# Three gated tiles with fewer convolution steps between them, the rest of the steps and the second output weight's split behind the last

## The chip, the cores and the metric

The kernel runs on one core of a Trainium2 chip. The metric is the device time of one execution in microseconds (us). The kernel before takes 1291.76 us, the median of three runs (1290.92 to 1293.04).

In this document PE is TensorE (the matrix engine), DVE is VectorE, ACT is ScalarE, POOL is GpSimd, and SP is the engine whose queue issues the loads and stores. "L553" is line 553 of the kernel.

## What is computed

A backbone of two layers works on 1024 tokens of width 1024. The change lies in the first layer, which has two branches behind one input projection, and one output projection behind both:

```python
z = h @ p["w_in"]
va, vg, ga, xb, gb = jnp.split(z, [W_CONV, 2 * W_CONV, 3 * W_CONV, 3 * W_CONV + W_LRU], axis=-1)
y_a = conformer_conv(va, vg, p) * jax.nn.silu(ga)      # 31 taps along the tokens, then a layernorm
y_b, hT = rglru_branch(xb, p, h0, True)                # two linear recurrences along the tokens
y_b = y_b * jax.nn.silu(gb)
return jnp.concatenate([y_a, y_b], axis=-1) @ p["w_out"], hT
```

The second layer (a pooling mixer) and the final norm follow. All of it is in 32-bit floating point, with each matrix product done as three products of a high and a low part (high by high, high by low, low by high).

## The kernel before, in words

**Tiles.** Channels lie on the 128 partitions, tokens along the free axis, so an activation of 1024 channels is 8 tiles (KT = 8) of 128 x 1024, and work goes by halves of 512 tokens. A weight tile is 128 x 1024: loaded raw from memory (`raw_load`, L579, by SP), rounded to its high part `wh` on ACT (`cast`), and subtracted to its low part `wl` on POOL (`gp`); both are in `raw_split` (L584). There are two buffers each for raw, high and low weights. A raw buffer comes free when POOL has made the low part from it.

**The stage of the change.** When the last recurrence has been scanned, its result for each tile n lies in memory (`yb_raw`). PE computes the gate products gb (weights gb4 to gb7 in this stage), 48 matmuls each (`gb_product`). ACT applies SiLU to each half (`gb_silu`, tiles `sb`). Then `gated(n, between)` (L1071) does, for each of the two halves of tile n: SP loads the half of the recurrence's result (`yr`, two buffers, so the load of a half waits until the multiplication two halves earlier is done); DVE multiplies it into the SiLU'd gate (`sb<-yr,sb`); ACT rounds the product to its high part (`ybh`); POOL subtracts to the low part (`ybl`); and DVE does `between` steps of the convolution (`fill(between)`). In this text half (n,h) is half h of tile n.

**The convolution's steps.** The convolution branch's 31 taps are DVE instructions, most of them `conv<-u,sm,conv`, cut into steps by a generator (`conv`, L617). Nothing but DVE is needed for them until the layernorm, so the code strews them between other work by `fill(n)`, n steps at a time. Seven steps follow each half of each output product (L1191), and before the last but one product is left, all steps still open are done (L1172), since the layernorm's mean needs all eight tiles.

**The output product.** From L1161 PE multiplies the gated tiles by the output weights wob0 to wob7, in order. Each is 24 matmuls per half: for each k of the 8 gated tiles, high weight by `ybh`, high weight by `ybl`, low weight by `ybh`. For wob0 the order is: k = 0 to 6 of half 0 (21 matmuls), k = 0 to 6 of half 1 (21), then k = 7 of half 0 and of half 1 (3 each). Its results leave by ACT (`wo`), are added on POOL to x (`xp`), and stored (`x_part`). After that come the layernorm, the products `ga` (gates of the convolution branch), and the second half of the output projection.

**What sets the order.** In this stage the order on PE, DVE, ACT and POOL is that of the program: each instruction is told to be issued behind the one before it on its engine (`on`, L549). The loads and stores on SP have no such order; a planner places them when it builds the program, by its own simulated time. From L1223 (`fixed[0] = False`) on, the order on all engines is the planner's.

The weights are split ahead of their use: in the loop at L1090, `gb_weights(j + 2)` splits gb6 and gb7 at j = 4 and 5, wob0 at j = 6 and wob1 at j = 7. The call stands ahead of `gated(j - 1)`, so the split of wob1 lies on ACT and POOL between the halves of tile 5 and those of tile 6.

Of the kernel before, what the change touches and what calls it, by code (L numbers as in the profile page):

```python
# [20 lines left out]
KT = D // P  # L21
# [35 lines left out]
def body(ctx, tc, xT, ctxT, cc, ccol, modT, modW, win, gw, wout, wu, grp, wg, wo1, small, edge, ident, outT):  # L57
# [501 lines left out]
    def cast(dst, src):  # L559
        return on("act", nc.scalar.copy, dst, src)  # L560

    def gp(*args, **kw):
        return on("pool", nc.gpsimd.tensor_tensor, *args, **kw)
# [15 lines left out]
    def raw_load(src, name):  # L579
        raw = wpool.tile([P, D], F32, tag="wr", name=f"wr_{name}")  # L580
        nc.sync.dma_start(raw, src)
        return raw

    def raw_split(raw, name):  # L584
        hi = wpool.tile([P, D], F32R, tag="wh", name=f"wh_{name}")
        lo = wpool.tile([P, D], F32R, tag="wl", name=f"wl_{name}")
        cast(hi, raw)
        gp(out=lo, in0=raw, in1=hi.bitcast(F32), op=sub)
        return hi, lo
# [14 lines left out]
    def vec(f, **kw):  # L604
        return on("vec", f, **kw) if fixed[0] else f(**kw)
# [56 lines left out]
    def ln_sums():  # L662
        for j in range(summed[0], ended[0]):
            for h in range(2):
                first = us[0][:, HALF[h]] if j == 1 else lnacc[h][:, :H]
                vec(nc.vector.tensor_tensor, out=lnacc[h][:, :H], in0=first, in1=us[j][:, HALF[h]], op=add)
        summed[0] = max(summed[0], ended[0])
# [24 lines left out]
    def fill(n):  # L692
        while n > 0:
            try:
                next(going[0])
                n -= 1
            except StopIteration:
                if begun[0] >= whole_[0]:
                    return
                going[0] = conv(begun[0])  # L700
                begun[0] += 1

    with ExitStack() as actx:
# [181 lines left out]
        def gb_weights(j):  # L885
            src, name = ((win[4 * KT + j], f"gb{j}") if j < KT else
                         (wout[j - KT, 1], f"wob{j - KT}") if j < 2 * KT else
                         (win[2 * KT + (0, KT // 2)[j - 2 * KT]], f"ga{(0, KT // 2)[j - 2 * KT]}"))
            gws[j] = raw_split(raw_load(src, name), name)

        def gb_product(j, w):
            if j == 4:
                gps[j] = (lambda t: [t[:, h] for h in HALF])(wide(f"gb{j}"))
            else:
                gps[j] = [psum(f"gb{j}_{h}") for h in range(2)]
            for h in range(2):
                all_of(mm3_fixed(gps[j][h], w, (hh, hl), HALF[h]))
# [3 lines left out]
        def gb_silu(j):  # L901
            sbs[j] = [ttile(f"sb{j}_{h}") for h in range(2)]
            for h in range(2):
                act(sbs[j][h], gps[j][h], AF.Silu)
# [32 lines left out]
    def d2tile(name, dt=F32):  # L937
        return d2pool.tile([P, S], dt, tag="d2", name=name)
# [5 lines left out]
    def vtile(name):  # L944
        return vpool.tile([P, H], F32, tag="v", name=name)
# [125 lines left out]
    def gated(n, between):  # L1071
        th, tl = d2tile(f"ybh{n}", F32R), d2tile(f"ybl{n}", F32R)
        for h in range(2):
            y = vtile(f"yr{n}_{h}")
            nc.sync.dma_start(y, yb_raw[n][:, HALF[h]])
            v = sbs[n][h]
            vec(nc.vector.tensor_tensor, out=v, in0=y, in1=v, op=mult)
            cast(th[:, HALF[h]], v)
            gp(out=tl[:, HALF[h]], in0=v, in1=th[:, HALF[h]].bitcast(F32), op=sub)
            fill(between)  # L1080
        bh.append(th)
        bl.append(tl)
# [7 lines left out]
    for j in range(3, KT + 1):  # L1090
        if j < KT:
            gb_silu(j)
        if 3 < j < KT:
            gb_weights(j + 2)
        if 3 < j < KT - 2:
            gb_product(j + 2, gws[j + 2])
        gated(j - 1, (0, 0, 4, 5, 5, 5, 3, 0)[j - 1])
        ln_sums()


# [809 lines left out]
```

## Time and profile before

| | |
|---|---|
| time, median of three runs | 1291.76 us |
| the profiled execution's own time | 1292.27 us |
| its span in the profile | 1290.5 us (1.77 us lie around it) |
| PE busy | 1264.4 us, 98% of the span |
| DVE busy | 1133.6 us, 88% |
| ACT, POOL busy | 648.8 us, 290.7 us |

A profile's page gives busy times of the engines. Further views of the trace are: the timeline, one row for each run of like instructions (start, duration, engine, line, what is written from what, count, and in brackets how long the engine had been idle and what released it); the table by stretches (busy time of each engine in a stretch of the span, with counts); the waits (who waited for whom, in all, how often, the longest); and the chain of waits that ended last, followed back from the last instruction. Helper functions record nearly all instructions of this stage under L553, so rows are told apart by the names of their tiles.

PE's matmuls are pipelined: where nothing holds them, their starts in this stage are 0.227 us apart, though each row shows a duration of 0.39 us.

### The profile page before, as it was taken

Reading aid. Unit: us, or ns where it says so; the run is one execution under the profiler, and the core shown is the slowest. Engines: PE = TensorE matmul, PEld = TensorE weight load, DVE = VectorE, ACT = ScalarE, POOL = GpSimd, SP = SyncE. Lnnn points to the kernel's source line nnn. Section 1 sums busy time; section 2 is a strip of 40 time slices with the busy share of each in tenths; the row PEclk is TensorE's granted clock in tenths of the full one; section 3 lists DMA queues with packets and bytes.
Section 4 is the critical chain, followed back from the end, with each engine's and each line's share of the span. In section 5 each row is a group of like instructions: output and inputs, shape, how many; then the busy total and the mean of one; then the engine's idle time right before and its main releaser. Section 6 shows DMA issues by size and latency. Waiting matters only on the chain.

```text
span 1290.5 us, 16117 instructions
## 1 busy us (share of the span) xinstructions
PE 1264.4 (98%) x5824; PEld 1040.4 (81%) x5824; DVE 1133.6 (88%) x1760; ACT 648.8 (50%) x939; POOL 290.7 (23%) x147
## 2 busy tenths in 40 slices
PE   9999999999999999999999999999999999999996
PEld 7788888888888887888887788787878888788785
DVE  6899999999999999969868959998999987887776
ACT  8555566656656533237434346644333444644542
POOL 0003464436443566434200032000000000000003
PEclk9999999999999999999999999999999999999998
DMA  9961121112111234442418566234333334868633
GB/s 374 396 211 49 42 74 43 64 41 74 57 66 57 82 115 137 143 137 82 163 50 285 173 212 177 92 123 155 117 115 120 115 122 131 298 225 281 212 110 130
DMA packets 78783, 182.33 MB, mean 141 GB/s; under 512 B 7664, under 2 KB 23408, under 8 KB 78704
## 3 DMA queue, kind: packets, MB, share of 16 engines
q1 hardware_dynamic: 70256, 177.12, 40.1%
q10 hardware_dynamic: 8448, 4.20, 1.1%
q8 instruction: 45, 0.74, 0.2%
q14 instruction: 34, 0.28, 0.1%
HBM read 137.24 MB, written 44.04 MB: 140 GB/s over the span
## 4 chain that ended last, share of the span: by engine, by line
PE 49%; DVE 31%; DMA 12%; issue 4%; ACT 3%; POOL 1%; SPq 0%; POOLq 0%; DVEq 0%; ACTq 0%
DVE conv L553 7%; PE wob L553 6%; PE vg L553 5%; PE va L553 5%; PE xb L553 4%; PE fold L123 3%; DVE l L553 3%; PE g L553 3%; DMA yr_t<-y_t 2%; DVE ws L1420 2%; DMA wr_v<-wfold 2%; PE ga L145 2%; PE ga L553 2%; PE ga L144 2%; PE ga L146 2%
## 5 line engine op out<-in xcount | busy, mean ns | idle before, releaser
L553 DVE SCALAR_TENSOR_TENSOR conv<-u,sm,conv 128x505 f32<-128x505 f32 (+6 forms) x224 | 153.5, 744 | 1.0
L1652 POOL TENSOR_TENSOR o<-x,rr 128x256 f32<-128x256 f32 (+1 forms) x10 | 9.9, 1022 | 448.7 <-ACT rr L1652 446.8
L553 ACT ACTIVATE l<-g,sm 128x512 f32<-128x512 f32 (+1 forms) x96 | 58.7, 619 | 57.8 <-PE g L553 57.0
L553 POOL TENSOR_TENSOR l<-l,l 128x1280 f32<-128x1280 f32 x16 | 47.1, 2966 | 25.6 <-DVE conv L553 14.1
L553 PE MATMUL wob<-ybl,wh_wob 128*128 128x512 f32 x128 | 50.2, 392 | 2.3 <-POOL ybl L553 2.3
L123 PE MATMUL fold<-gh,wh_wu 128*128 128x512 f32 x128 | 51.1, 399 | 1.2 <-ACT wh_wu L103 1.2
L103 ACT CAST wq_g<-wr_g 128x512 fp32r<-128x512 f32 x48 | 28.2, 620 | 46.6 <-DMA wr_g<-wg 15.0
L123 PE MATMUL fold<-gh,wl_wu 128*128 128x512 f32 x128 | 50.2, 395 | 0.5 <-DVE wl_wu L104 0.5
L553 PE MATMUL gb<-h0h,wl_gb 128*128 128x512 f32 x128 | 49.9, 390 | 0.3 <-POOL wl_gb L553 0.3
L123 PE MATMUL fold<-gl,wh_wu 128*128 128x512 f32 x128 | 50.1, 391 | 0.0
L553 PE MATMUL va<-h0h,wl_va 128*128 128x512 f32 x128 | 49.9, 390 | 0.1
L553 PE MATMUL vg<-h0h,wl_vg 128*128 128x512 f32 x128 | 49.9, 390 | 0.0
L553 PE MATMUL wob<-ybh,wl_wob 128*128 128x512 f32 x128 | 49.8, 389 | 0.0
L553 PE MATMUL gb<-h0l,wh_gb 128*128 128x512 f32 x128 | 49.8, 389 | 0.0
L553 PE MATMUL gb<-h0h,wh_gb 128*128 128x512 f32 x128 | 49.8, 389 | 0.0
L553 PE MATMUL va<-h0l,wh_va 128*128 128x512 f32 x128 | 49.8, 389 | 0.0
L553 PE MATMUL va<-h0h,wh_va 128*128 128x512 f32 x128 | 49.8, 389 | 0.0
L553 PE MATMUL wob<-ybh,wh_wob 128*128 128x512 f32 x128 | 49.8, 389 | 0.0
L553 PE MATMUL vg<-h0h,wh_vg 128*128 128x512 f32 x128 | 49.8, 389 | 0.0
L553 PE MATMUL vg<-h0l,wh_vg 128*128 128x512 f32 x128 | 49.8, 389 | 0.0
L553 DVE TENSOR_TENSOR_SCAN l<-l,l 128x256 f32<-128x256 f32 (+1 forms) x32 | 48.7, 1522 | 1.1
L553 DVE SCALAR_TENSOR_TENSOR conv<-cL,wsum,conv 128x506 f32<-128x506 f32 (+3 forms) x70 | 48.1, 744 | 0.2
(596 smaller groups left out, 4272.5 us busy)
## 6 DMA issues: line engine op xcount, KB each, us to landing
wr_wu<-wu SPq DMA_DIRECT2D x16, 512.0 KB, 4.2
modw<-modW SPq DMA_DIRECT2D x16, 512.0 KB, 10.2
x_part<-xp SPq DMA_DIRECT2D x32, 256.0 KB, 2.3
mod<-modT SPq DMA_DIRECT2D x32, 256.0 KB, 3.7
wr_v<-wfold SPq DMA_DIRECT2D x16, 512.0 KB, 4.1
wr_g<-wg SPq DMA_DIRECT2D x16, 512.0 KB, 4.8
wr_wo<-wo SPq DMA_DIRECT2D x16, 512.0 KB, 4.5
yr_t<-y_t SPq DMA_DIRECT2D x16, 512.0 KB, 5.8
```

The source lines that it names most:

```text
L103: return (nc.scalar.copy(hi, src), eng.tensor_tensor(out=lo, in0=src, in1=hi.bitcast(F32), op=sub))
L123: m = nc.tensor.matmul(*args, **kw)
L144: mm(ps, hi[:, kc], xh[k][:, cols], start=(k == 0), stop=False)
L145: mm(ps, hi[:, kc], xl[k][:, cols], start=False, stop=False)
L146: mm(ps, lo[:, kc], xh[k][:, cols], start=False, stop=(k == ks - 1))
L553: last[eng] = f(*args, **kw)
L1420: nc.vector.tensor_tensor(out=nxt[:, :, a_:b_], in0=cur[:, :, a_ + o0 : b_ + o0], in1=cur[:, :, a_ + o1 : b_ + o1], op=add)
L1652: tail[eng] = f(*args, **kw)
```

## The change

```diff
     for j in range(3, KT + 1):
         if j < KT:
             gb_silu(j)
-        if 3 < j < KT:
+        if 3 < j < KT - 1:
             gb_weights(j + 2)
         if 3 < j < KT - 2:
             gb_product(j + 2, gws[j + 2])
-        gated(j - 1, (0, 0, 4, 5, 5, 5, 3, 0)[j - 1])
+        gated(j - 1, (0, 0, 4, 5, 5, 3, 1, 0)[j - 1])
+        if j == KT:
+            gb_weights(KT + 1)
+            fill(8)
         ln_sums()
```

Three steps instead of five follow each half of tile 5, one instead of three each half of tile 6: eight steps fewer. Behind the last half of tile 7 stand the load and split of wob1 (which were ahead of tile 6) and the eight steps. Nothing is computed that was not computed before, and nothing is left out; the instructions' number on each engine stays the same.

## The prediction

> **What bounds the kernel now.** I read the page first, then the table by stretches around the stage of the change, then the waits, then the timelines of PE, DVE, ACT, POOL and SP from 485 to 512 us, and last the chain behind it. The page and the table:
>
> ```profile
> span 1290.5 us, 16117 instructions
> PE 1264.4 (98%) x5824; PEld 1040.4 (81%) x5824; DVE 1133.6 (88%) x1760; ACT 648.8 (50%) x939; POOL 290.7 (23%) x147
> ...
> 440.00:499.70 59.70, 59.43 (x262) 48.89 (x262) 57.60 (x82) 20.49 (x32) 29.21 (x17) 1.00 0.36 115
> 499.70:512.00 12.30, 10.01 (x42) 7.30 (x41) 12.09 (x19) 4.16 (x6) 8.24 (x7) 1.00 0.36 116
> 512.00:675.00 163.00, 163.00 (x720) 134.91 (x720) 132.76 (x202) 69.89 (x105) 52.99 (x29) 1.00 0.35 117
> ```
>
> The columns of the table are the stretch, its length, then busy time of PE, weight loads, DVE, ACT, POOL, and the granted clock. PE is the bound: 59.43 of 59.7 us before the start of the output product's trouble, and 163.00 of 163.00 behind it. Between the two lie 12.3 us in which it is busy for 10.01. The waits of 440 to 540 us name what it waits for, and PE's timeline shows where:
>
> ```profile
> PE wob L553 <- POOL ybl L553: 2.3, 3, 1.6
> ```
>
> ```profile
> 495.69 0.39 PE L553 MATMUL wob<-ybh,wh_wob 128*128 128x512 f32 x1
> 499.77 0.39 PE L553 MATMUL wob<-ybh,wh_wob 128*128 128x512 f32 x1
> 501.75 0.50 PE L553 MATMUL wob<-ybl,wh_wob 128*128 128x512 f32 x1 [1.59 <-POOL ybl L553]
> 507.14 0.39 PE L553 MATMUL wob<-ybh,wh_wob 128*128 128x512 f32 x1
> 507.94 0.50 PE L553 MATMUL wob<-ybl,wh_wob 128*128 128x512 f32 x1 [0.42 <-POOL ybl L553]
> 509.19 0.51 PE L553 MATMUL wob<-ybl,wh_wob 128*128 128x512 f32 x1 [0.28 <-POOL ybl L553]
> 511.82 0.39 PE L553 MATMUL wob<-ybh,wh_wob 128*128 128x512 f32 x1
> ```
>
> Number the matmuls of the output product. The one at 495.69 is the 1st; the one at 499.77 is the 19th (k = 6 of half 0, high by high). Eighteen pitches in 4.08 us are 0.2267 us each. The 20th needs the low part of half (6,0) and starts at 501.75 instead of 500.00. The 43rd (k = 7) starts at 507.14; by the pitch it would have been 495.69 + 42 x 0.2267 = 505.21, so the first wait has cost **1.93**. The 44th and 47th wait for the low parts of (7,0) and (7,1). The 58th, at 511.82, would have been at 508.61: **3.21 us** are lost in all, 1.28 of them by the last two waits. This is more than the 2.3 us of idle, because the matmuls behind each wait also start at a wider spacing for a while. 3.21 us is all that the stage has to give.
>
> **Why the low parts are late.** The rows of DVE (the `sb` rows are the multiplications of halves (5,1), (6,0), (6,1) and, two in one row, (7,0) and (7,1)), then ACT, then POOL:
>
> ```profile
> 489.07 3.51 DVE L553 SCALAR_TENSOR_TENSOR conv<-u,sm,conv 128x511 f32<-128x511 f32 x5
> 492.49 0.74 DVE L553 TENSOR_TENSOR sb<-yr,sb 128x512 f32<-128x512 f32 x1
> 493.15 3.35 DVE L553 SCALAR_TENSOR_TENSOR conv<-u,sm,conv 128x508 f32<-128x508 f32 x5
> 496.42 0.68 DVE L553 TENSOR_TENSOR sb<-yr,sb 128x512 f32<-128x512 f32 x1
> 497.02 2.30 DVE L553 SCALAR_TENSOR_TENSOR conv<-u,sm,conv 128x507 f32<-128x507 f32 x3
> 499.24 1.34 DVE L553 TENSOR_TENSOR sb<-yr,sb 128x512 f32<-128x512 f32 x1
> 500.50 1.23 DVE L553 SCALAR_TENSOR_TENSOR edge_junk<-u,sm 128x8 f32<-128x8 f32 x1
> 501.76 1.73 DVE L553 TENSOR_TENSOR u<-u 128x512 f32<-128x512 f32 x1
> ...
> 505.18 1.29 DVE L553 TENSOR_TENSOR sb<-yr,sb 128x512 f32<-128x512 f32 x2
> ```
>
> ```profile
> 495.95 0.60 ACT L553 ACTIVATE sb<-gb 128x512 f32<-128x512 f32 x1 [1.57 <-PE gb L553]
> 496.44 1.04 ACT L553 CAST wh_wob<-wr_wob 128x1024 fp32r<-128x1024 f32 x1
> 497.39 0.62 ACT L553 CAST ybh<-sb 128x512 fp32r<-128x512 f32 x1
> ```
>
> ```profile
> 497.62 2.40 POOL L553 TENSOR_TENSOR wl_wob<-wr_wob,wh_wob 128x1024 fp32r<-128x1024 f32 x1 [2.36 <-ACT wh_wob L553]
> 499.97 2.98 POOL L553 TENSOR_TENSOR ybl<-sb,ybh 128x512 fp32r<-128x512 f32 x2
> 506.60 2.53 POOL L553 TENSOR_TENSOR ybl<-sb,ybh 128x512 fp32r<-128x512 f32 x2 [3.65 <-ACT ybh L553]
> ```
>
> The first wait is the second weight's: its cast (1.04) stands on ACT ahead of `ybh` of (6,0), and its subtraction (2.40) on POOL ahead of `ybl` of (6,0), which so starts at 499.97 and not near 497.1. The other two are the convolution's: three steps, the last of them spread over 500.50 to 505.18, hold the multiplication of (7,0) until 505.18, so its low part starts at 506.60.
>
> **The change, walked through.** Up to 489.07 nothing moves. A step is 3.51 / 5 = 0.70 us, a multiplication takes about 0.65 of DVE's time. All times below are estimates from the rows above.
>
> DVE: three steps to 491.2, multiplication of (5,1) to 491.8, three steps to 493.9, (6,0) to 494.5, a step to 495.2, (6,1) to 495.9, a step to 496.6. Then a wait that was not there before: `yr` of (7,0) can be loaded only when (6,0) has freed its buffer.
>
> ```profile
> DMA to landing us min/median/max: 2.5/2.8/4.3
> ```
>
> ```profile
> 483.37 0.33 SPq L581 DMA_DIRECT2D wr_wob<-wout  x1
> 491.45 0.33 SPq L581 DMA_DIRECT2D wr_wob<-wout  x1
> ...
> 510.86 0.33 SPq L1107 DMA_DIRECT2D x_part<-xp  x1
> ```
>
> The first row is that of the `yr` tile: 2.8 us from issue to landing, 4.3 at most. So (7,0) starts at 494.5 + 2.8 = 497.3 and ends at 498.0; (7,1), whose load is issued at 495.9, starts at 498.7 and ends at 499.4 (with two slow loads, 500.9). DVE stands idle for 0.7 + 0.7 us (2.9 with slow loads). Behind the waiting multiplications stand only convolution steps, for which nobody waits before 560 us. On SP the load at 491.45 (the third weight, held there for its buffer) is ahead of 491.8, so it does not hold the `yr` loads up.
>
> ACT: the SiLU at 495.95 waits for PE's last gate product, as now; the next instruction starts at 496.45, and this is now `ybh` of (6,0), done at 497.05; (6,1) at 497.6, (7,0) at 498.65, (7,1) at 500.05, then the second weight's cast, to 501.1.
>
> POOL, at 1.30 us a half (2.53 / 2 rounded up): (6,0) from 497.1 to 498.4, (6,1) to 499.7, (7,0) to 501.0, (7,1) to 502.3, then the second weight's low part, 2.40, to 504.7.
>
> PE, without a wait: low of (6,0) asked for at 500.00 (1.6 us spare), (7,0) at 505.4 (4.4 spare), (7,1) at 506.1 (3.8 spare), the second weight's high part at 506.6 (5.5 spare), its low part at 507.0 (2.3 spare). With the slow `yr` loads (7,1)'s low part ends near 502.9 and the weight's at 505.3, still 1.7 early. **So all three waits go: -3.21.**
>
> The second weight's raw load is issued at 483.37 now, when its buffer comes free. The change leaves the buffer's time as it is, but the planner may put the load later on SP. Behind the last `yr` load it would be issued near 496.3, land 3.9 us later by this tile's median (row below), and be cast by 501.3: POOL comes free for it only at 502.3. From nothing to nothing, then; I take zero.
>
> ```profile
> DMA to landing us min/median/max: 3.4/3.9/4.8
> ```
>
> **The moved steps.** Eight steps of 0.70 are 5.6 us of DVE work, done 5 to 15 us later, plus 1.4 to 2.9 us of new idle. DVE works without a gap until the convolution ends, and then:
>
> ```profile
> 566.69 3.37 DVE L553 TENSOR_TENSOR ml_mu<-lnsum,mh_mu 128x512 fp32r<-128x512 f32 x2 [9.92 <-ACT mh_mu L553]
> ...
> 654.68 0.69 DVE L1277 TENSOR_TENSOR u<-u,ga 128x512 f32<-128x512 f32 x1 [4.14 <-ACT ga L1275]
> ```
>
> The steps cost nothing, because this idle of 9.92 us stands at their end. PE asks 3.2 us sooner and DVE arrives up to 2.9 later, so 3.8 or more remain. If that cover were gone, each microsecond beyond it would be a microsecond of PE. Behind that point DVE follows PE again (the 4.14 at 654.68 waits on a SiLU of a product of PE), and the chain of waits runs over PE alone from 509 to here, and then through ACT and DVE instructions that this matmul releases:
>
> ```profile
> 674.57 0.24 PE ga L145
> ```
>
> So what PE gains at 509 us is still there at 675, and the work behind starts as much earlier.
>
> **A rule weighed against the rows.** The multiplication of (6,1) takes 1.34 us beside a POOL subtraction, where that of (6,0) takes 0.68; `u<-u`, which reads two tiles, takes 1.73. The change packs four subtractions, two multiplications and a weight's subtraction together. If each waits for the other's end here, as those rows suggest, the order is: (6,0) low to 498.4, multiplication (7,0) to 499.1, (6,1) low to 500.4, multiplication (7,1) to 501.1, (7,0) low to 502.4, (7,1) low to 503.7, the weight to 506.1, or 506.8 with `u<-u` between. PE asks at 507.0. The sum stays 3.2, but with 0.2 us to spare instead of 2.3; it is the ground of the first rival. The Trainium skill, page "SBUF — State Buffer", section "SBUF: two separate sides", has this as a rule: DVE and GpSimd share one port pair as an exclusive lock, and against a DVE instruction with two inputs in SBUF the one that starts first keeps it while the other stands still. The rows agree with it, and by it the alternation is the case to expect; it speaks against the change.
>
> **The sum.** 1292.27 (the profiled execution's time) - 3.21 = 1289.06. The median of the runs shown, 1291.76, lies 0.51 under that execution, and 1291.76 - 3.21 = **1288.55, forecast 1288.6**. About 0.2% (2.6 us, from 1291.76 to 1289.2) is what a measurement of this kernel can tell from no change, so the forecast lies just outside.
>
> **The rivals.**
>
> *The second weight is late by a little* (chance 0.13). The alternation above together with slow `yr` loads (1.5 us more) puts its low part near 508.2; PE waits 1.2, and the spacing behind the wait adds some 0.3, as behind 501.75. Then 1.7 of 3.2 remain: **1290.1**. For it: the 1.34 and 1.73 rows. Against: it needs both together.
>
> *The planner lays out the free part anew* (0.15). From L1223 on the order is not written down. A simulated shift of PE against SP's loads can change what stands first there, and single waits on loads behind 675 us are 3 to 6 us in the chain (6.20 for `cH<-cc` at 695.33). So -3.2 and up to 6 either way: **1283 to 1294**, a third of it in each class. Against: behind 566 us all engines follow PE, so a shift common to all should leave the order alone.
>
> ```profile
> 695.33 6.20 DMA cH<-cc
> ```
>
> *The second weight's load is placed far back on SP* (0.08): slower. If the planner puts it behind the first result's store (510.86 now, 507.7 after the gain), it lands at 508.0 + 3.9 = 511.9, is cast by 513.0 and split by 515.4. PE stands from 507.0 to 515.4: 8.4 lost against 3.2 gained, **1297.0**. It begins to cost when the load is issued after about 499.6 (507.0 - 2.4 - 1.04 - 3.9), and the whole is slower from about 502.8. Against: SP is idle when the buffer comes free at 483.
>
> **How the numbers follow.** Forecast 0.64, rivals 0.13, 0.15, 0.08. The forecast's own spread is 1287.8 to 1289.6 (the runs before lie within about 1 us of their median), so about 0.55 of its 0.64 is faster by over 0.2% and 0.09 within. The first rival gives 0.01, 0.11, 0.01 (faster, same, slower), the planner 0.05, 0.05, 0.05, the late load 0.08 slower. In all: faster 0.61, same 0.25, slower 0.14. The range 1286.0 to 1293.0 holds the forecast, the first rival and the middle of the planner's spread; outside lie the late load (0.08) and about 0.09 of the planner.
>
> **What would show it.** Right: in PE's timeline no idle in brackets on the `wob` rows, the 58th matmul 12.9 us behind the 1st; on POOL four `ybl` in a row from about 497.1, then `wl_wob`; on DVE one or two waits for `yr` of about 0.7 us; the idle before `ml_mu` at 4 to 6 us; the `ga` products ending near 671.4. Wrong: a `wob` row that waits for `wl_wob` (the first and third rivals), a raw load of the second weight issued after 499.6, or the stage 3.2 us shorter and the span not (the second).

## The result, and the profile after

| | before | changed |
|---|---|---|
| median of 19 runs | 1291.64 us | 1288.31 us |
| all runs | 1288.59 to 1294.17 us | 1285.04 to 1293.57 us |
| ratio, 95% interval | | 0.9978 [0.9968, 0.9988] |
| the profiled execution's time, span | 1292.27, 1290.5 us | 1292.66, 1290.9 us |

The change is worth 3.33 us by the medians; 1288.6 was forecast. The recorded ratio, 0.9978, is 2.8 us, and its interval 1.5 to 4.1 us, so it is partly luck that the median came within 0.3 us of the forecast. The profiled execution of the changed kernel happens to be one of its longer ones, so the two spans say nothing; the stage has to be read. First the table by stretches of the changed kernel (stretch, length, busy time of PE, weight loads, DVE, ACT, POOL, granted clock):

```profile
440.00:500.00 60.00, 59.73 (x264) 49.11 (x263) 57.20 (x79) 20.80 (x33) 29.93 (x18) 1.00 0.36 119
500.00:512.00 12.00, 12.00 (x55) 9.94 (x54) 11.69 (x18) 3.88 (x5) 10.53 (x7) 1.00 0.42 138
512.00:671.00 159.00, 159.00 (x703) 131.62 (x702) 137.07 (x205) 69.78 (x104) 50.44 (x28) 1.00 0.34 116
```

PE, which stood 2.3 of 12.3 us, is now busy in all 12.00 us of its stretch. Its timeline has no bracket on the output product. The rows are the 1st, the 20th, 44th and 47th (those that waited) and the 58th matmul, and the last one of the gate products `ga`:

```profile
495.81 0.39 PE L553 MATMUL wob<-ybh,wh_wob 128*128 128x512 f32 x1
...
500.11 0.39 PE L553 MATMUL wob<-ybl,wh_wob 128*128 128x512 f32 x1
...
505.55 0.39 PE L553 MATMUL wob<-ybl,wh_wob 128*128 128x512 f32 x1
...
506.23 0.39 PE L553 MATMUL wob<-ybl,wh_wob 128*128 128x512 f32 x1
...
508.73 0.39 PE L553 MATMUL wob<-ybh,wh_wob 128*128 128x512 f32 x1
...
671.54 0.39 PE L146 MATMUL ga<-h0h,wl_ga 128*128 128x512 f32 x1
```

The stage, from the 1st to the 58th, takes 508.73 - 495.81 = 12.92 us where it took 16.13. In the kernel before, the same last gate product stood here:

```profile
674.63 0.39 PE L146 MATMUL ga<-h0h,wl_ga 128*128 128x512 f32 x1
```

That is 178.94 us behind the 1st matmul before, and 671.54 - 495.81 = 175.73 now. **3.21 us are saved in the stage and 3.21 are still there 160 us later.** DVE, POOL and ACT of the changed kernel, in that order:

```profile
491.25 0.80 DVE L553 TENSOR_TENSOR sb<-yr,sb 128x512 f32<-128x512 f32 x1
...
493.93 1.07 DVE L553 TENSOR_TENSOR sb<-yr,sb 128x512 f32<-128x512 f32 x1
494.93 0.74 DVE L553 SCALAR_TENSOR_TENSOR conv<-u,sm,conv 128x509 f32<-128x509 f32 x1
495.82 0.69 DVE L553 TENSOR_TENSOR sb<-yr,sb 128x512 f32<-128x512 f32 x1 [0.15 <-DMA yr<-yb_raw]
496.43 0.74 DVE L553 SCALAR_TENSOR_TENSOR conv<-u,sm,conv 128x507 f32<-128x507 f32 x1
497.76 1.33 DVE L553 TENSOR_TENSOR sb<-yr,sb 128x512 f32<-128x512 f32 x1 [0.58 <-ACT ybh L553]
499.33 1.46 DVE L553 TENSOR_TENSOR sb<-yr,sb 128x512 f32<-128x512 f32 x1 [0.24 <-DMA yr<-yb_raw]
...
542.18 1.90 DVE L553 SCALAR_TENSOR_TENSOR edge_junk<-u,sm 128x8 f32<-128x8 f32 x1
...
545.83 1.86 DVE L553 SCALAR_TENSOR_TENSOR conv<-u,wsum 128x512 f32<-128x512 f32 x1
...
559.75 1.29 DVE L553 TENSOR_TENSOR lnsum<-lnsum,u 128x512 f32<-128x512 f32 x2
563.59 3.38 DVE L553 TENSOR_TENSOR ml_mu<-lnsum,mh_mu 128x512 fp32r<-128x512 f32 x2 [2.55 <-ACT mh_mu L553]
```

```profile
497.25 5.96 POOL L553 TENSOR_TENSOR ybl<-sb,ybh 128x512 fp32r<-128x512 f32 x4 [2.79 <-ACT ybh L553]
503.15 2.41 POOL L553 TENSOR_TENSOR wl_wob<-wr_wob,wh_wob 128x1024 fp32r<-128x1024 f32 x1
```

```profile
496.56 1.13 ACT L553 CAST ybh<-sb 128x512 fp32r<-128x512 f32 x2
...
501.35 1.05 ACT L553 CAST wh_wob<-wr_wob 128x1024 fp32r<-128x1024 f32 x1
```

The reader sees the walk of the prediction: the high parts of tile 6 right behind the SiLU, four `ybl` in a row from 497.25, then the weight's low part, done at 505.56 against the 507.1 at which PE takes it. And one number that is not as forecast: DVE stands idle for 2.55 us ahead of `ml_mu`, no longer 9.92.

On PE the order of the instructions is the same in both kernels from first to last. On DVE, ACT and POOL only the moved instructions stand elsewhere, and on SP one later weight load stands behind two loads of x instead of ahead of them: the planner left the free part as it was.

### The profile page after: what moved, and what is told of

The parts are those of the page before. It is cut to its first block, busy times and chain, and to the rows that moved or that the text cites. A ratio compares the mean times of both kernels' runs of the same rounds, so it can differ in the third digit from the quotient of the medians.

```text
span 1290.9 us, 16117 instructions
## 1 busy us (share of the span) xinstructions
PE 1265.5 (98%) x5824; PEld 1041.8 (81%) x5824; DVE 1137.1 (88%) x1760; ACT 649.7 (50%) x939; POOL 290.2 (22%) x147
## 4 chain that ended last, share of the span: by engine, by line
PE 55%; DVE 26%; DMA 11%; issue 3%; ACT 2%; POOL 1%; SPq 0%; POOLq 0%; DVEq 0%; ACTq 0%
PE wob L553 7%; PE fold L123 7%; PE vg L553 5%; PE va L553 5%; DVE conv L553 5%; PE xb L553 4%; DVE l L553 3%; PE g L553 3%; DVE ws L1423 2%; PE ga L553 2%; PE ga L144 2%; PE ga L145 2%; PE gb L553 2%; PE ga L146 2%; PE xbc L553 2%
```

## The experiments

**Theory:** the three waits are set by the order on ACT, POOL and DVE. The second weight's split causes the first, the steps cause the other two, and the moved work is free as long as DVE's idle ahead of the layernorm's mean lasts. **Rivals:** one of the two parts is the whole cause; the waits are chance; DVE has slack without limit. The measure is the stage, since it was the same within 0.01 us in both profiles of each kernel, while the totals of one kernel spread over 5 to 9 us. A total below is a median, against the median of the kernel before in the same series of runs; the ratio beside it is the recorded one, with its interval, and not the quotient of the two medians.

**Both kernels once more**, unchanged, for a second profile of each.

> The kernel before once more, for a second profile. My theory (the three waits are set by the order on the engines): the same three waits within 0.1 us, stage 16.1. Rival (the waits are chance, as the total's spread of some 5 us between runs might suggest): they differ by more than 0.5 us. Behind the stage I expect the same work to take up to 4 us more or less, by where the granted clock falls.

> The changed kernel once more, for a second profile. My theory: no wait in the stage, 12.9 us, gate products ending 175.7 us behind its start, and the work behind them takes another time than the 610.4 us of the first profile, since that profile had a stretch at 0.62 of the clock near 1217 us. Rival (the change costs time behind the gate products): again about 4 us more behind them than in the kernel before (606.7).

The kernel before, second profile:

```profile
501.94 0.50 PE L553 MATMUL wob<-ybl,wh_wob 128*128 128x512 f32 x1 [1.59 <-POOL ybl L553]
...
508.13 0.50 PE L553 MATMUL wob<-ybl,wh_wob 128*128 128x512 f32 x1 [0.45 <-POOL ybl L553]
...
509.38 0.50 PE L553 MATMUL wob<-ybl,wh_wob 128*128 128x512 f32 x1 [0.29 <-POOL ybl L553]
```

The same three waits within 0.03 us, stage 16.13 again. The changed kernel: no wait, 12.92, gate products at 175.75. The waits are no chance. From the last gate product to PE's last matmul the kernel before took 606.7 and 609.8 us in its two profiles, the changed one 610.4 and 608.8. A spread of 3 us lies there, on both sides; over all ten profiles of this text it is 606.0 to 610.9. Two profiles of each kernel can't say whether the change costs something there. The totals can: their interval, 1.5 to 4.1 us gained, holds the whole 3.21.

**The weight alone**: the old counts of steps, the split behind the last tile.

```diff
-        gated(j - 1, (0, 0, 4, 5, 5, 3, 1, 0)[j - 1])
+        gated(j - 1, (0, 0, 4, 5, 5, 5, 3, 0)[j - 1])
         if j == KT:
             gb_weights(KT + 1)
-            fill(8)
```

> Only the split of the second output weight goes behind the last gated tile; five and three convolution steps stay between the tiles. The measure is the stage: from the start of the 1st matmul of the output product to the start of the 58th, 16.13 us in the kernel before (495.69 to 511.82) and 12.92 in the changed one (495.81 to 508.73). My theory (the first wait is the weight's, the other two the steps'): the first wait goes (1.93), the low part of (6,0) ends near 499.1; the steps still hold the multiplication of (7,0) to about 502 to 505, so its low part and the weight's behind it come 0.3 to 2 us late. Stage 14.0 to 15.5, total 1289.5 to 1291. Rival (the weight is the whole cause, since its subtraction on GpSimd also slows the vector engine's steps beside it): no wait is left, stage 12.9, total as the changed kernel's, 1288.3. Second rival (the steps are the whole cause, the vector engine being the one that is late): stage stays at 16.1.

PE's waits in its output product:

```profile
506.58 0.50 PE L553 MATMUL wob<-ybl,wh_wob 128*128 128x512 f32 x1 [0.16 <-POOL ybl L553]
...
508.92 0.50 PE L553 MATMUL wob<-ybh,wl_wob 128*128 128x512 f32 x1 [1.13 <-POOL wl_wob L553]
```

Stage 14.81 us, 1.32 less than before; total 1291.24 against 1291.88, ratio 0.9988 [0.9974, 1.0002]. The first wait is gone. But tile 7 still comes late, and the weight stands behind it on POOL, so the weight's own low part is what PE waits for now. DVE shows one thing more. Its order is that of the kernel before, and still it reaches the multiplications of tile 7 sooner:

```profile
499.97 0.16 DVE L553 SCALAR_TENSOR_TENSOR edge_junk<-u,sm 128x8 f32<-128x8 f32 x1
...
500.18 0.69 DVE L553 TENSOR_TENSOR u<-u 128x512 f32<-128x512 f32 x1
...
502.56 1.28 DVE L553 TENSOR_TENSOR sb<-yr,sb 128x512 f32<-128x512 f32 x2
```

In the kernel before, the same rows took 1.23 and 1.73, and tile 7 started at 505.18. So the split on POOL, and the low parts that it made late, had also held up the steps, by 2.6 us: the rival's mechanism is real, only its claim that no wait is left is wrong.

**The steps alone**: the new counts of steps and the eight behind, the split in its old place.

```diff
-        if 3 < j < KT - 1:
+        if 3 < j < KT:
             gb_weights(j + 2)
...
         if j == KT:
-            gb_weights(KT + 1)
             fill(8)
```

> Only the convolution steps move (three and one between the tiles, eight behind the last); the second weight's split stays ahead of tile 6. My theory: the low part of (6,0) still stands behind the weight's subtraction (497.6 to 500.0), so the first wait stays at its 1.93 us; the low parts of tile 7 are then ready at about 505.2 while the matrix engine asks for them at 507.3, so the other two waits go (1.28). Stage 14.85, total about 1290.4. Rival (the weight is the whole cause): stage 16.1, total 1291.6. Second rival (the steps are the whole cause): stage 12.9, total 1288.3.

```profile
501.87 0.50 PE L553 MATMUL wob<-ybl,wh_wob 128*128 128x512 f32 x1 [1.58 <-POOL ybl L553]
```

One row in PE's output product has a bracket, the first wait. Stage 14.84 us (14.85 expected), total 1292.17 against 1291.88, ratio 0.9997 [0.9985, 1.0009]. The totals of these two runs can't tell 1.3 us from none; the stages do, and both rivals with one cause fall: they asked for 12.9 in one run and 16.1 in the other. The two parts alone save 1.32 + 1.29 = 2.61, together 3.21: either alone leaves or makes a wait that the other removes.

**No steps at all between the halves of tiles 5 and 6**, sixteen behind the last tile.

```diff
-        gated(j - 1, (0, 0, 4, 5, 5, 3, 1, 0)[j - 1])
+        gated(j - 1, (0, 0, 4, 5, 5, 0, 0, 0)[j - 1])
         if j == KT:
             gb_weights(KT + 1)
-            fill(8)
+            fill(16)
```

> The changed kernel with no convolution step at all between the halves of tiles 5 and 6, and sixteen instead of eight behind the last tile. My theory (3.21 us were all that the stage had, and no wait is left in it): stage 12.9 as in the changed kernel, total equal to the changed kernel's within noise, 1287 to 1290; the vector engine waits 2 to 4 us for the loads of the recurrence's result and reaches the layernorm's mean later by as much, against 2.55 us that it stood idle ahead of it, so a loss of 0 to 1.5 us at that mean is the risk. Rival (the gated tiles still set the pace, fewer steps between them are better still): stage the same but total lower by another 1 to 3 us.

The first block is PE's, the second DVE's:

```profile
508.88 0.39 PE L553 MATMUL wob<-ybh,wh_wob 128*128 128x512 f32 x1
...
570.91 0.80 PE L553 MATMUL mu<-mh_mu,ones_r 128*128 128x512 f32 x1 [4.08 <-ACT mh_mu L553]
```

```profile
530.27 4.05 DVE L553 TENSOR_TENSOR lnsum<-lnsum,u 128x512 f32<-128x512 f32 x2
...
552.80 2.83 DVE L553 TENSOR_TENSOR u<-u 128x512 f32<-128x512 f32 x1
...
569.46 1.29 DVE L553 TENSOR_TENSOR lnsum<-lnsum,u 128x512 f32<-128x512 f32 x2
```

The stage is 12.93, so there is indeed nothing left in it. But PE stands 4.08 us at the layernorm's mean, the gate products end 181.80 us behind the 1st matmul, and the total is 1295.88 against 1291.88, ratio 1.0025 [1.0007, 1.0044]: **slower than the kernel before.** My expectation of 0 to 1.5 us of loss there was too small by far; 6.07 were lost (181.80 - 175.73): the wait of 4.08, and behind it a stretch from 571 to 574 in which the granted clock was 0.50. DVE waits 3.7 us for loads of `yr` in the stage (two waits; three of 0.97 in all in the changed kernel), and the sums `lnsum` end 9.6 us later behind the 1st matmul than in the changed kernel (570.75 and 561.04 on the two clocks). Waiting is the smaller part of that. The larger is DVE instructions that take longer here, beside a POOL instruction: the first two `lnsum` together 4.05 us instead of 1.28, `u<-u` 2.83 instead of 0.69.

**Needless DVE work behind the last tile**, twelve instructions and, in a second run (`range(3)`), three, added to the changed kernel.

```diff
             fill(8)
+            for _ in range(12):
+                vec(nc.vector.tensor_tensor, out=us[0][:, HALF[0]], in0=us[0][:, HALF[0]], in1=us[0][:, HALF[0]],
+                    op=ALU.max)
```

> The changed kernel with twelve needless instructions on the vector engine behind the last gated tile (each takes the larger of a half tile and itself, about 0.60 us, so 7.2 us in all). My theory (the moved steps were free because the vector engine stood idle ahead of the layernorm's mean, 2.55 us in the changed kernel's profile): the first 2.55 us are covered and the rest reaches the matrix engine at the mean, where it stands 4.6 us or somewhat more; the clock granted to it may fall behind that, as behind the 4.08 us in the run without steps between, which adds some 2 us. Stage 12.9, last matmul of the gate products 4.6 to 7 us later than 175.7 us behind the start of the stage, total 1293 to 1295. Rival (the vector engine has slack all along, as its idle in later stages suggests): total as the changed kernel's, 1288.3.

> As the run with twelve needless instructions, but with three (1.8 us, more if they meet a GpSimd instruction). My theory: 1.8 us is under the 2.55 us of idle, so the matrix engine does not wait at the mean, the idle there falls to about 0.7 us, and the last matmul of the gate products stays 175.7 us behind the start of the stage; total as the changed kernel's. Rival (every added microsecond of the vector engine costs a microsecond, since the chain of waits runs over its convolution steps ahead of the stage): 1.8 us later, total 1290.1.

Twelve: DVE's row of the added work, then PE's at the mean.

```profile
508.72 15.86 DVE L553 TENSOR_TENSOR u<-u 128x512 f32<-128x512 f32 x12
```

```profile
574.00 0.79 PE L553 MATMUL mu<-mh_mu,ones_r 128*128 128x512 f32 x1 [7.39 <-ACT mh_mu L553]
```

Three: the same two views.

```profile
509.03 5.31 DVE L553 TENSOR_TENSOR u<-u 128x512 f32<-128x512 f32 x3
```

```profile
567.53 0.51 PE L553 MATMUL mu<-ml_mu,ones_r 128*128 128x512 f32 x1 [0.38 <-DVE ml_mu L553]
```

Both expectations missed the size of the added work: beside POOL the instructions took 1.3 and 1.8 us each instead of 0.60, and with three PE did wait, 0.38 us. Stages 12.92 in both. With twelve, the gate products end at 186.47, 10.74 later than in the changed kernel, and the total is 1299.21 against 1293.14, ratio 1.0051 [1.0034, 1.0068]. With three, `lnsum` ends 3.39 us later than in the changed kernel, measured from the 1st matmul (564.66 - 496.04 against 561.04 - 495.81), and the gate products 0.82 later (176.55): 2.57 us were covered, and 2.55 was the idle that the profile showed. Total 1291.68 against 1293.14, ratio 0.9985 [0.9968, 1.0002]. So the rivals fall on both sides: the slack is neither without limit nor nothing.

**The split later still**, behind the first result's eviction.

```diff
         if j == KT:
-            gb_weights(KT + 1)
             fill(8)
...
             wob_evict(m, h)
+            if (m, h) == (0, 0):
+                gb_weights(KT + 1)
             fill(7)
```

> The changed kernel with the second weight's load and split put still later, behind the first result's eviction (first half of the first output). My theory (a split costs from the moment its end passes the matmul that asks for it): the cast stands behind the eviction at 506.3 and ends near 508.0, the subtraction behind the first result's addition ends near 510.7; the matrix engine asks for the high part at 506.7 and for the low part at 507.1, so it stands about 1.3 and then 2.4 us, 3.6 to 4 in all. Stage 16.5 to 17, total 1291.5 to 1293, as slow as before the change. Rival (the matrix engine has slack here, or the place of the split does not matter once it is out of the tiles' way): stage 12.9, total 1288.3.

```profile
507.85 0.50 PE L553 MATMUL wob<-ybh,wh_wob 128*128 128x512 f32 x1 [1.09 <-ACT wh_wob L553]
...
510.61 0.79 PE L553 MATMUL wob<-ybh,wl_wob 128*128 128x512 f32 x1 [2.02 <-POOL wl_wob L553]
...
513.76 0.63 PE L553 MATMUL wob<-ybh,wh_wob 128*128 128x512 f32 x1
```

Two waits where expected, for the weight's high and then its low part, 3.1 us in all. The stage is 18.04, longer than the 16.5 to 17 expected, because the matmuls behind 510.61 stand 0.43 us apart: the granted clock was 0.50 from 511 to 515. By the last gate product 6.3 us are lost against the changed kernel (182.05 and 175.73 behind the 1st matmul). The total is 1294.48, above the 1291.5 to 1293 expected, against 1291.88, ratio 1.0011 [0.9997, 1.0026]; it can't be told from the kernel before. SP issues the load at 483.38, as in the changed kernel, so only the split has moved. The place of the split does matter: the point from which it costs is that of the mechanism in the prediction's third rival, the time at which PE asks for it.

## Why the prediction was right

- **What the stage has to give, 3.21 us:** 16.13 - 12.92 = 3.21, measured in two profiles of each kernel.
- **Which part causes which wait:** the first wait stays at 1.58 with the steps alone and goes with the weight alone. Forecast as 1.93 and 1.28; the parts alone save 1.32 (weight) and 1.29 (steps). The 1.28 was right. The weight alone did not save 1.93, since its own low part then comes too late. And the other two waits were not the steps' alone, as the prediction had it: with the split moved and the steps left, 0.16 us of them remained, since three DVE instructions ahead of tile 7 were shorter.
- **The times of the walk:** POOL's four halves from 497.25 (497.1 forecast), but 1.49 us each on average (5.96 / 4) instead of 1.30, so they ended at 503.2 and the weight at 505.56, not 502.3 and 504.7. The spare of 2.3 us was 1.6. DVE's last four multiplications took 1.07, 0.69, 1.33 and 1.46 instead of 0.65. This is the alternation that was weighed against the rows; by that the weight was to end at 506.1 or later, so the truth lay between. The Trainium skill, page "SBUF — State Buffer", section "SBUF: two separate sides", says that a DVE instruction with two inputs in SBUF and a GpSimd instruction that reads SBUF hold a shared port pair one at a time. The longer rows of both engines agree with it.
- **DVE's new idle:** 1.0 us in three brackets against 1.4 forecast. The longest names ACT, but it too ends with a load of `yr`: that load is issued at 495.03, and at the changed kernel's median of 2.7 us to landing it arrives at 497.7, just ahead of the multiplication at 497.76.
- **The cover was mis-sized.** The prediction took 9.92 us of idle ahead of `ml_mu`, 3.2 off for PE's gain and up to 2.9 for DVE's lateness, and kept 3.8 or more (4 to 6 in its last part). 2.55 remained. In the kernel before, three rows of DVE stood so:

```profile
539.65 0.16 DVE L553 SCALAR_TENSOR_TENSOR edge_junk<-u,sm 128x8 f32<-128x8 f32 x1
...
541.56 0.76 DVE L553 SCALAR_TENSOR_TENSOR conv<-u,wsum 128x512 f32<-128x512 f32 x1
...
554.38 2.39 DVE L553 TENSOR_TENSOR lnsum<-lnsum,u 128x512 f32<-128x512 f32 x2
```

DVE reached the end of `lnsum` at 556.77 then and at 561.04 now, 4.3 later. Of these 2.5 stand already at the first `lnsum` row (520.90 then, 523.44 now); only 1.0 of them is idle. (The eight moved steps themselves took 8.2 us there, 500.71 to 508.88, not 5.6.) The other 1.7 come behind it. The term left out is what a shift does to some DVE instructions: the 8-element `edge_junk` takes 1.90 us now and 0.16 before, `conv<-u,wsum` 1.86 and 0.76, since POOL's work now lies beside them, in these two rows of the changed kernel; `lnsum` went the other way (1.29 now, 2.39 before).

```profile
541.66 2.40 POOL L553 TENSOR_TENSOR wl_wob<-wr_wob,wh_wob 128x1024 fp32r<-128x1024 f32 x1
...
545.85 1.29 POOL L553 TENSOR_TENSOR xp<-xp,wo 128x512 f32<-128x512 f32 x1 [1.78 <-issue]
```

That POOL's work is the cause is shown by the run with the weight alone, where the order on DVE was unchanged and `edge_junk` took 0.16 instead of 1.23 in the stage, and 1.18 at 537.02, where POOL works from 536.89 to 538.18. The forecast time survived because 2.55 is still above zero, and as far as the left-out term goes, that is luck. The run with no steps between shows what the same term does when the cover is gone.

- **The way to the end:** 3.21 us still stood at the last gate product, the planner kept its order, and the medians moved by 3.33.
- **The rivals:** the weight late by a little did not come; nor did the free part laid out anew or the load placed far back (it is issued at 483.43). The late split shows what the third one would cost, PE standing for the second weight, but there the order on ACT and POOL was the cause and not a late load.

## What to carry to other kernels

When the busiest engine waits at the start of a product, ask for each operand which queue brought it late: here two parts of one edit removed two causes that acted on each other, and either alone was worth less than half. Work that is moved out of the way is free only as far as the idle at its new deadline reaches; measure that idle after the move, since a shift also changes which instructions of DVE and POOL collide. And where totals spread by more than the effect, measure the stage from one fixed instruction to another.

## What was not expected of the hardware

**A wait of PE can cost well over its length.** In the run with the late split 3.1 us of idle cost 18.04 - 12.92 = 5.1 by the 58th matmul and 6.3 by the last gate product; in the run with twelve needless instructions a wait of 7.39 cost 10.74. The table by stretches of the first run, then of the second (the figure behind POOL's count in brackets is the granted clock):

```profile
507.00:511.00 4.00, 1.13 (x3) 0.69 (x4) 3.93 (x7) 2.32 (x3) 4.00 (x3) 0.78 0.18 66
511.00:515.00 4.00, 4.00 (x10) 3.08 (x10) 4.00 (x7) 0.00 (x0) 3.14 (x2) 0.50 0.76 257
```

```profile
574.00:580.00 6.00, 6.00 (x13) 4.43 (x14) 5.67 (x10) 4.28 (x7) 1.28 (x1) 0.50 0.14 47
```

Behind the idle the clock is granted at half, until about 516 and 580 us in these two runs (5 to 6 us from PE's next matmul) and for some 3 us in the run without steps between. In that time a matmul starts every 0.43 instead of 0.227 us.

**A short wait can bring the clock down, and need not.** In the kernel before, the clock fell elsewhere in its profile, behind a wait of 2.00 us; in its second profile behind one of 1.80; in the changed kernel's profile near 1217, behind three waits of which none reached 0.8 us. The rows in that order:

```profile
717.26 0.54 PE L1021 MATMUL qc_woa<-ya_t1h,wq_woa 128*128 128x512 f32 x1 [2.00 <-DVE wq_woa L104]
```

```profile
756.40 0.50 PE L123 MATMUL fold<-gh,wh_wu 128*128 128x512 f32 x1 [1.80 <-ACT wh_wu L103]
```

```profile
1211.61 0.50 PE L1020 MATMUL qc_wo<-y_b22l,wq_wo 128*128 128x512 f32 x1 [0.76 <-DVE y_b22l L104]
...
1213.83 0.72 PE L1018 MATMUL qb_wo<-y_t4h,wq_wo 128*128 128x512 f32 x1 [0.79 <-ACT y_t4h L103]
1215.09 0.79 PE L1020 MATMUL qb_wo<-y_t4l,wq_wo 128*128 128x512 f32 x1 [0.54 <-DVE y_t4l L104]
```

It also fell near 1120 us in the kernel before's second profile (behind 2.94 us) and near 809 in the changed kernel's (1.86 and 0.90). It did not fall behind 1.90 us at 717.59 in the kernel before's second profile, nor behind 2.17 at 1113.19 in the changed kernel's first, nor behind the waits of 1.6 us that the change removes, in any of the three profiles that have them. The Trainium skill, page "TensorE: Matmul & The Clock Gate", section "What's actually happening", describes a gate with a free-running window of about 3.4 us that halves the clock after at least one idle window. The runs agree with the half, and a window that runs free of the program would explain the chance, though no run here shows the window itself. The length does not agree: no wait in the rows above is as long as such a window, and the measurement decides.

These stretches are part of the spread between executions of one kernel: 6 to 13 matmuls at 0.43 us in each, which by the difference to 0.227 is an estimated loss of 1.4 to 2.8 us. They are not all of it. With this estimate taken off, the time from the last gate product to PE's last matmul is 605.1 and 605.7 us in the two profiles of the kernel before, and 607.6 and 607.4 in those of the changed one. What makes the rest was not looked into; by the 95% interval of the totals at most 1.7 us of it (3.21 - 1.5) can be the change's.
